# Gate loads four chunks sooner, and sparse work paced over the output phase's first chunks too

## The chip, the cores and the metric

The kernel runs on one core of one Trainium2 chip, as one launch. The metric is device microseconds of that launch. Three runs of the kernel before took 1379.41, 1379.86 and 1382.35 us; their median is 1379.86 us. All arithmetic is in float32 (matmuls on split float32r parts).

## The reference, cut to what matters

One encoder block: a mixer (gated convolution beside a recurrent scan), then a product-key expert layer, then a final normalization. The change lies wholly in the expert layer:

```python
def block(xb):                                  # 128 tokens at a time, 512 in all
    q = (xb @ w_q).reshape(p, PEER_HEADS, 2, PEER_DK_HALF)
    sc = jnp.einsum('phcd,hcnd->phcn', q, sub_keys)
    top_s, top_i = lax.top_k(sc, PEER_TOPK)
    ...
    g = jax.nn.softmax(best_s, axis=-1)
    u_sel = expert_u[idx]
    act = jax.nn.gelu(jnp.einsum('phkd,pd->phk', u_sel, xb), approximate=False)
    coef = (g * act.astype(jnp.float32)).astype(xb.dtype)
    return jnp.einsum('phk,phkd->pd', coef, expert_v[idx])
```

There are 16384 experts, and each token selects 128 of them (8 heads, 16 each). `expert_u` and `expert_v` have 16384 rows of 1024 numbers, 64 MB each.

## The kernel before

**Two ways to the experts.** The last 320 of the 512 tokens are done densely: every expert's activation is computed by matmul, in chunks of 128 experts. `u` chunk c gives `act` for those 320 tokens (24 matmuls of 320 columns, three per 128 rows of the model dimension since both sides are split into a high and a low part). `v` chunk n multiplies the coefficients of its 128 experts, 384 tokens wide, with 128 rows of `expert_v` (18 matmuls of 512 columns: three token blocks, two halves of the output, three split products) and accumulates over all 128 chunks in PSUM. The first 128 tokens (and, for the `u` side, 64 more) are done sparsely: for each of 128 selections a gather on GpSimd's queue (`gath`, L804-L807) fetches one expert row per token, 512 KB in all, into a ring of row buffers, and VectorE makes of it a dot product (`dots`, L828, on the `u` side) or a weighted sum (`sums`, L844, on the `v` side). One such instruction with its gather is a sparse step here. The ring has 5 buffers, and two more from some point in the output phase (`row_tile`, L795-L799), so gathers run four to six rows ahead of the step that uses them.

**Gates.** The softmax weights of the dense tokens are scattered beforehand into per-tile DRAM arrays `Gd[1..3]`, and `v` chunks read them back, 16 chunks at a time: three loads of 1 MB each, in pieces of 1 KB, one per token tile t (`load_g16`, L922-L937). The chunks 0 to 15 use a buffer `gt`. The chunks 16 to 31 use the memory of `h2`, the split normalized activations that the `u` chunks read; it is free once the last `u` chunk has been multiplied. The later groups of 16 alternate between the two.

**The order of the work.** The kernel writes the order out by hand, job by job. A list `jobs` holds `u` chunks 0 to 123, then `v0, u124, v1, u125, v2, u126, v3, u127, v4, v5, ...` (L852-L856). What follows `u123` is called the output phase here; its loop is L1104-L1131. At job k it asks for the weight chunk of job k+5 (`w_load`, 512 KB on SyncE's queue, the tile `wraw`, four buffers), splits the chunk of k+3 into its high part on ScalarE (`w_high`, the tile `whi`, L75) and of k+2 into its low part on VectorE (`w_low`, the tile `wlo`, L80); in a `v` job it then calls `v_gates(n + 5)` for the gates, on even n `v_act` and `v_gated` (L962, the coefficients `cf` of the next chunk pair, their high part `ch` on ScalarE), on odd n `v_rest` (the low part `cl` on VectorE, L980), issues the 18 matmuls, and last some sparse steps. The queue of SyncE is worked off in order, as are ScalarE and VectorE. Every weight load waits for the buffer's last reader, the `w_low` four jobs before it.

**When the gates are asked for.** `v_gates(n)` starts, for tile t, the load of the group that begins at chunk m = n + 4 - t while n < 16, and m = n + 13 - 3t after that (L951). For the group that begins at 16 this is at n = 13, 14 and 15, so in the jobs of the chunks 8, 9 and 10.

**How many sparse steps.** After `v` chunk n, steps are taken until their number reaches `share` (L1128). With 207 steps still to do at the loop's start (`steps`), NE = 128, VE = 1, QV = 3 and RB = 32 it is

share = min(max(n + 1 - 3, 0) / 124, 1) x (207 + 0.31 x 96) - 0.31 x max(n - 31, 0),

so none in the first three chunks, then a constant number per chunk, and 0.31 fewer per chunk from chunk 32 on, where spilled activations are loaded back too.

Of the kernel before, what the change touches and what calls it, by code (L numbers as in the profile page):

```python
# [21 lines left out]
NE = 128  # L22
# [12 lines left out]
def block_kernel(ctx, tc, xT, small, w_ada1, w_ada, b_ada, w_in, w_r, w_i, w_out, w_q, keys, uT, u, v, final_g, out):  # L35
# [825 lines left out]
    def w_load(k):  # L861
        if k < len(jobs):
            kind, i = jobs[k]
            if 5 <= k < FN:
                raw = wring.tile([128, KB, 128], FR, name=("wlo", "whi")[k % 2], bufs=WB).bitcast(F32)
                nc.sync.dma_start(raw, uT[i])
                wraw[k] = raw
                return
            wraw[k] = load_w(uT[i] if kind == "u" else
                             v[vorder[i] * 128:(vorder[i] + 1) * 128, :].rearrange("p (k e) -> p k e", k=KB))  # L870

    def w_high(k):
        if FN <= k < len(jobs):
            whi[k] = high(wraw[k])

    def w_low(k):
        if FN <= k < len(jobs):
            wlo[k] = low(wraw.pop(k), whi[k])
# [14 lines left out]
    def u_evict():  # L893
        if unread:
            c, ps = unread.pop()
            if c % 2 == 0:
                act[c // 2] = ring.tile([128, 2, NU], F32, name="act", bufs=RB // 2)
            nc.scalar.activation(act[c // 2][:, c % 2], ps, AF.Gelu)  # L898

    def u_chunk(k, pool):  # L900
        c = jobs[k][1]
        if c:
            ps = pool.tile([128, NU], F32, name="ps_act", bufs=2)
            if k < FN:
                raw = wraw.pop(k)
                for j in range(KB):
                    nc.tensor.matmul(ps, raw[:, j, :], h2f[j // 2][:, j % 2], start=j == 0, stop=j == KB - 1)
            else:
                mm3(ps, whi.pop(k), wlo.pop(k), hd, ld, range(KB), True, True)
            u_evict()  # L910
            unread.append((c, ps))
        q = c // 2 - RB // 2 + 2
        if c % 2 == 0 and 0 <= q < v0 // 2:
            spill(q)
        pe[0] += FPE if c and k < FN else 3530
        dve[0] += 0 if c and k < FN - 2 else 1140
        ac[0] += 450 if c and k < FN - 3 else 1400
# [4 lines left out]
    def load_g16(m, t):  # L922
        if m not in g16:
            if m % 32:
                big = g16[16] if m > 16 else persist.tile([128, 32, 16, 16], F32, name="h2")[:, 0:NG]
            else:
                big = gt8.rearrange("p s g i t -> p (s g i t)").rearrange("p (g i t) -> p g i t", i=16, t=16)
            g16[m] = big
            for k in range(0, 16, 2):
                gbuf[m + k] = big[:, :, k:k + 2, :]  # L930
        for k in range(0, 16, 8):
            cc = vorder[m + k]
            if k == 0 and vorder[m + 8] == cc + 8:
                nc.sync.dma_start(g16[m][:, 8 * t - 8:8 * t], Gd[t][:, :, cc:cc + 16, :].rearrange("g j i t -> j g i t"))
                return
            nc.sync.dma_start(g16[m][:, 8 * t - 8:8 * t, k:k + 8],
                              Gd[t][:, :, cc:cc + 8, :].rearrange("g j i t -> j g i t"))  # L937

    def v_gates(n):
        if n >= NE or n in gdone:  # L940
            return
        gdone.add(n)
        cc = vorder[n]
        if n < 16 and n % 8 == 0:
            gt = gt8[:, n // 8]
            for t in (2, 3, 1):
                nc.sync.dma_start(gt[:, 8 * t - 8:8 * t], Gd[t][:, :, cc:cc + 8, :].rearrange("g j i t -> j g i t"))
            for k in range(0, 8, 2):
                gbuf[n + k] = gt[:, :, k:k + 2, :]
        for t in range(1, NT):  # L950
            m = n + (4 - t if n < 16 else 13 - 3 * t)  # L951
            if m >= 16 and m % 16 == 0 and m < NE:
                load_g16(m, t)

    def v_act(q):
        if q < NE // 2:
            c = vorder[2 * q] // 2
            if act[c] is None:
                act[c] = ring.tile([128, 2, NU], F32, name="act", bufs=RB // 2)
                nc.sync.dma_start(act[c].rearrange("p c t -> p (c t)"), Ad[c])  # L960

    def v_gated(q):  # L962
        if q < NE // 2:
            cf = vp.tile([128, 2, ND], F32, name="cf", bufs=1)
            g = gbuf.pop(2 * q)
            nb = XB // 16
            nc.scalar.activation(cf[:, :, 0:XB].rearrange("p c (g t) -> p c g t", t=16),
                                 g[:, 0:nb].rearrange("p g c t -> p c g t"), AF.Copy)
            nc.vector.tensor_mul(cf[:, :, XB:].rearrange("p c (g t) -> p c g t", t=16),  # L969
                                 act.pop(vorder[2 * q] // 2).rearrange("p c (g t) -> p c g t", t=16),  # L970
                                 g[:, nb:].rearrange("p g c t -> p c g t"))
            ch = vp.tile([128, 2, ND], FR, name="ch", bufs=2)
            nc.scalar.activation(ch, cf, AF.Copy)  # L973
            coef[q] = (cf, ch)

    def v_rest(q):
        if q < NE // 2:
            cf, ch = coef[q]
            cl = vp.tile([128, 2, ND], FR, name="cl", bufs=2)
            nc.vector.tensor_sub(cl, cf, ch.bitcast(F32))  # L980
            coef[q] = (ch, cl)
# [36 lines left out]
    for k in range(CE):  # L1018
# [13 lines left out]
        while dve[0] < RHO * pe[0] or k == KD:  # L1032
# [7 lines left out]
            n = next(gens[g], 0)  # L1040
# [20 lines left out]
        m = k - CE + XE  # L1061
        if 0 <= m < XE:
            for n in [0] if m < 2 else range(5) if m == XE - 1 else [8]:
                v_gates(n)
# [17 lines left out]
    def v_chunk(n, b):  # L1082
        hi, lo, ch, cl = vsp[n]
        bs = slice(b * 128, (b + 1) * 128)
        for st, mv, first, last in ((ch, hi, n == 0, False), (ch, lo, False, False), (cl, hi, False, n == NE - 1)):
            for e in range(2):
                nc.tensor.matmul(accs[b][e], st[:, bs], mv[:, e * 512:(e + 1) * 512], start=first, stop=last)  # L1087
# [15 lines left out]
    steps, done = len(usteps) - len(bdone) + 128, 0  # L1103
    for k in range(CE, len(jobs)):  # L1104
        w_load(k + 5)
        w_high(k + 3)
        w_low(k + 2)
        kind, n = jobs[k]
        if kind == "u":
            u_chunk(k, psP)  # L1110
        else:
            q, e = divmod(n, 2)
            v_gates(n + 5)
            if e == 0:
                v_act(q + 4)
                v_gated(q + 1)
            else:
                v_rest(q + 1)
            vsp[n] = [w.pop(k).rearrange("p k e -> p (k e)") for w in (whi, wlo)] + [c[:, e] for c in coef[q]]
            if n < NE - VT:  # L1120
                for b in range(3):
                    v_chunk(n, b)
                del vsp[n]
            u_evict()
            pe[0] += 4090
            dve[0] += 2005
        if kind == "v":
            share = min(max(n + 1 - QV, 0) / (NE - VE - QV), 1) * (steps + 0.31 * (NE - RB)) - 0.31 * max(n + 1 - RB, 0)  # L1128
            while done < share and next(sparse, None):
                done += 1  # L1130
    fin = vp.tile([128, 2, 3, D], F32, name="gt", bufs=1)  # L1131
# [50 lines left out]
VE = 1  # L1182
# [5 lines left out]
CE = 124  # L1188
GB_E = 5
DR = 1.1  # L1190
QU = 6
QV = 3
RB = 32
ZL = 1
XE = 5
# [52 lines left out]
```

## Time and profile before

| | us |
|---|---|
| median of three runs | 1379.86 |
| the profiled execution | 1382.99 |
| its span, first to last instruction | 1381.1 |
| TensorE busy | 1325.2 (96%) |
| VectorE busy | 1222.7 (89%) |
| ScalarE busy | 700.7 (51%) |
| GpSimd busy | 528.9 (38%) |
| HBM read and written | 393.54 MB and 45.09 MB, 318 GB/s over the span |
| first matmul of `v` chunk 0 | 808.75 |

The profile is one execution. "Idle before" is time in which an engine did nothing ahead of an instruction, and the name behind the arrow is what that instruction waited for last. Matmuls are pipelined, each recorded longer than the distance to the next, so TensorE's loss is read from the distances and not from its busy share. "DMA share" is the busy time of packets over 16 DMA engines; it goes a little over 1 where packets overlap. q0 is the queue of GpSimd's gathers, q1 that of SyncE's loads and stores. In this profile and in what follows, `h` is the tile name under which the memory of `h2` appears.

### The profile page before, as it was taken

How to read it: one execution, taken by the hardware profiler on the slowest of the kernel's cores; microseconds unless marked ns; L12 is line 12 of the kernel's file. 1: busy time of each engine (PE TensorE's matmuls, PEld its weight loads, DVE VectorE, ACT ScalarE, POOL GpSimd, SP SyncE). 2: the span in 40 equal slices, each digit the busy share in tenths (PEclk: the TensorE clock that was granted, in tenths of full speed). 3: DMA queues.
4: the chain of work that ended last, by engine and by line, in shares of the span. 5: the costliest groups of instructions: out<-in, count | busy, mean ns of one | idle time of the engine just before them, and what ended most of it. 6: DMA issues, size and time to landing. Idle time of an engine off the chain costs nothing.

```text
span 1381.1 us, 21224 instructions
## 1 busy us (share of the span) xinstructions
PE 1325.2 (96%) x7483; PEld 1126.6 (82%) x7483; DVE 1222.7 (89%) x2302; ACT 700.7 (51%) x1199; POOL 528.9 (38%) x334
## 2 busy tenths in 40 slices
PE   5999999999999999999999999899999999999995
PEld 2666787777989999999999998787878887787884
DVE  6887766989999999999998649799999989898998
ACT  4666635424686887788644343333343434343442
POOL 0000000000242543435423406577656667576760
PEclk9999999999999999999999999999999999999998
DMA  9776332250699999999999988999999999999994
GB/s 352 253 265 217 126 93 99 69 184 31 215 317 347 343 412 331 363 334 407 417 397 336 406 260 283 407 393 416 413 414 412 415 413 414 411 415 412 409 377 164
DMA packets 146926, 440.03 MB, mean 319 GB/s; under 512 B 14722, under 2 KB 42370, under 8 KB 144772
## 3 DMA queue, kind: packets, MB, share of 16 engines
q1 hardware_dynamic: 99812, 267.75, 52.1%
q0 software_dynamic: 46720, 169.89, 31.4%
q8 instruction: 58, 0.95, 0.3%
q10 hardware_dynamic: 288, 1.05, 0.2%
q14 instruction: 48, 0.39, 0.1%
HBM read 393.54 MB, written 45.09 MB: 318 GB/s over the span
## 4 chain that ended last, share of the span: by engine, by line
DVE 32%; PE 21%; issue 21%; DMA 18%; ACT 4%; POOL 2%; DVEq 0%; SPq 0%; POOLq 0%; ACTq 0%
DMA wraw<-in_v_dram 14%; DVE wlo L80 7%; DVE scr L828 6%; PE ps_z L89 5%; PE ps_z L90 5%; PE ps_z L91 5%; DVE ys L844 3%; DMA wraw<-in_uT_dram 2%; DVE oh L667 2%; POOL rows L807 2%; DVE cf L969 2%; DVE cl L980 2%; ACT whi L75 1%; ACT igh L683 1%; PE ps_row L135 1%
## 5 line engine op out<-in xcount | busy, mean ns | idle before, releaser
L75 ACT ACTIVATE whi<-wraw 128x1024 fp32r<-128x1024 f32 x281 | 297.1, 1057 | 357.7 <-DMA wraw<-in_v_dram 192.8
L80 DVE TENSOR_TENSOR wlo<-wraw,whi 128x1024 fp32r<-128x1024 f32 x281 | 342.9, 1220 | 84.3 <-ACT whi L75 83.3
L89 PE MATMUL ps_act<-h,whi 128*128 128x320 f32 x928 | 293.8, 317 | 5.6 <-ACT act L898 5.6
L91 PE MATMUL ps_act<-h,wlo 128*128 128x320 f32 x928 | 288.1, 310 | 0.8 <-DVE wlo L80 0.8
L90 PE MATMUL ps_act<-h,whi 128*128 128x320 f32 x928 | 288.0, 310 | 0.0
L807 POOL DMA_INDIRECT rows<-in_u_dram,idx_s x128 | 192.5, 1504 | 213.6 <-DVE scr L828 183.4
L807 POOL DMA_INDIRECT rows<-in_v_dram,idx_s x128 | 225.5, 1762 | 107.4 <-DVE ys L844 82.5
L1087 PE MATMUL acc<-whi,ch 128*128 128x512 f32 x750 | 233.0, 392 | 7.6 <-ACT ch L973 7.1
L1087 PE MATMUL acc<-whi,cl 128*128 128x512 f32 x750 | 233.4, 392 | 5.7 <-DVE cl L980 5.6
L1087 PE MATMUL acc<-wlo,ch 128*128 128x512 f32 x750 | 231.9, 390 | 0.0
L807 POOL DMA_INDIRECT rows<-in_u_dram,idx_b x64 | 105.7, 1651 | 235.0 <-DVE scr L828 112.2
L89 PEld LDWEIGHTS ps_act<-h,whi 128*128 128x128 f32 x928 | 175.6, 189 | 7.8 <-ACT act L898 6.6
L91 PEld LDWEIGHTS ps_act<-h,wlo 128*128 128x128 f32 x928 | 175.4, 189 | 1.0 <-DVE wlo L80 1.0
L90 PEld LDWEIGHTS ps_act<-h,whi 128*128 128x128 f32 x928 | 175.6, 189 | 0.2
L1087 PEld LDWEIGHTS acc<-whi,ch 128*128 128x128 f32 x750 | 140.8, 189 | 39.0 <-ACT ch L973 9.4
L1087 PEld LDWEIGHTS acc<-whi,cl 128*128 128x128 f32 x750 | 140.3, 188 | 39.5 <-DVE cl L980 10.8
L1087 PEld LDWEIGHTS acc<-wlo,ch 128*128 128x128 f32 x750 | 141.4, 189 | 29.7
L844 DVE SCALAR_TENSOR_TENSOR ys<-rows,acts,ys 128x1024 f32<-128x1024 f32 x127 | 162.7, 1281 | 1.7
L828 DVE SCALAR_TENSOR_TENSOR scr<-rows,h2n 128x1024 f16<-128x1024 f32 x128 | 156.2, 1221 | 1.7 <-DMA rows<-in_u_dram,idx_s 0.2
L898 ACT ACTIVATE act<-ps_act 128x320 f32<-128x320 f32 x127 | 54.9, 432 | 139.5 <-PE ps_act L91 101.6
L683 ACT ACTIVATE igh<-oh,gl 128x128 f16<-128x128 f16 x320 | 99.7, 432 | 20.7 <-DVE oh L667 20.5
L433 POOL DMA_DIRECT2D x1d<-xn x8 | 4.5, 569 | 258.5 <-ACT xn L432 258.5
(284 smaller groups left out, 1837.2 us busy)
## 6 DMA issues: line engine op xcount, KB each, us to landing
wraw<-in_v_dram SPq DMA_DIRECT2D x128, 512.0 KB
wraw<-in_uT_dram SPq DMA_DIRECT2D x121, 512.0 KB
Gd<-stg SPq DMA_DIRECT2D x46, 512.0 KB
wada<-in_w_ada_dram SPq DMA_DIRECT2D x16, 1024.0 KB
Ad<-act SPq DMA_DIRECT2D x48, 320.0 KB
act<-Ad SPq DMA_DIRECT2D x48, 320.0 KB
h<-Gd SPq DMA_DIRECT2D x12, 1024.0 KB
wraw<-in_w_in_dram SPq DMA_DIRECT2D x20, 512.0 KB
```

The source lines that it names most:

```text
L75: nc.scalar.activation(hi, raw, AF.Copy)
L80: nc.vector.tensor_sub(lo, raw, hi.bitcast(F32))
L89: nc.tensor.matmul(ps, hi[:, k, :], xh(k), start=first and k == ks[0], stop=False)
L90: nc.tensor.matmul(ps, hi[:, k, :], xl(k), start=False, stop=False)
L91: nc.tensor.matmul(ps, lo[:, k, :], xh(k), start=False, stop=last and k == ks[-1])
L667: nc.vector.tensor_tensor(flat.rearrange("p (q n b) -> p q n b", q=8, b=2), io2[:, None, :, :].to_broadcast(shp), sij[:, a0].rearrange("p ...
L683: nc.scalar.activation(ig[:, 1, k // 2, :, k % 2], of[:, k // 2, 0, :, k % 2], AF.Copy, scale=gl[:, t0 + k:t0 + k + 1])
L807: nc.gpsimd.indirect_dma_start(out=r[:, :], out_offset=None, in_=table, in_offset=bass.IndirectOffsetOnAxis(ap=idxs[:, k:k + 1], axis=0))
L828: nc.vector.scalar_tensor_tensor(scr, rows.pop(n), 1.0, hn, op0=OP.mult, op1=OP.mult, accum_out=dst[:, k:k + 1])
L844: nc.vector.scalar_tensor_tensor(ys, rows.pop(k), acts[:, k:k + 1], ys, op0=OP.mult, op1=OP.add)
L898: nc.scalar.activation(act[c // 2][:, c % 2], ps, AF.Gelu)
L1087: nc.tensor.matmul(accs[b][e], st[:, bs], mv[:, e * 512:(e + 1) * 512], start=first, stop=last)
```

## The change

The gates for chunks 16 to 31, which go into the memory of `h2`, are asked for at n = 9, 10 and 11, so in the jobs of the chunks 4, 5 and 6. The group's later successors are asked for where they were. The sparse share begins with chunk 0; while a `u` chunk still stands between two `v` chunks (the first NE - CE = 4), each chunk counts as 1.86, and the whole counts 127 + 0.86 x 4 = 130.44.

```diff
         for t in range(1, NT):
-            m = n + (4 - t if n < 16 else 13 - 3 * t)
+            m = n + (8 - t if n < 16 else 13 - 3 * t)
             if m >= 16 and m % 16 == 0 and m < NE:
                 load_g16(m, t)
...
         if kind == "v":
-            share = min(max(n + 1 - QV, 0) / (NE - VE - QV), 1) * (steps + 0.31 * (NE - RB)) - 0.31 * max(n + 1 - RB, 0)
+            paced = n + 1 + UV * min(n + 1, NE - CE)
+            share = min(paced / (NE - VE + UV * (NE - CE)), 1) * (steps + 0.31 * (NE - RB)) - 0.31 * max(n + 1 - RB, 0)
             while done < share and next(sparse, None):
                 done += 1
...
-QV = 3
+UV = 0.86
```

The order of TensorE's instructions does not change. On SyncE, at the start of the output phase, the queue before reads (`wraw` are weight chunks, `h` the memory of `h2`, `Gd` the gates in DRAM, `gt` the other gate buffer):

```order
L70 DMA wraw<-in_uT_dram 128x1024
L70 DMA wraw<-in_v_dram 128x1024 x10
L934 DMA h_9519<-Gd_2592 128x8x256
L70 DMA wraw<-in_v_dram 128x1024
L934 DMA h_9519<-Gd_2593 128x8x256
L70 DMA wraw<-in_v_dram 128x1024
L934 DMA h_9519<-Gd_2594 128x8x256
L70 DMA wraw<-in_v_dram 128x1024 x7
L934 DMA gt<-Gd_2592 128x8x256
```

After the change the same stretch, from the same last `u` load to the same `gt` load, reads:

```order
L70 DMA wraw<-in_uT_dram 128x1024
L70 DMA wraw<-in_v_dram 128x1024 x6
L934 DMA h_9424<-Gd_2592 128x8x256
L70 DMA wraw<-in_v_dram 128x1024
L934 DMA h_9424<-Gd_2593 128x8x256
L70 DMA wraw<-in_v_dram 128x1024
L934 DMA h_9424<-Gd_2594 128x8x256
L70 DMA wraw<-in_v_dram 128x1024 x11
L934 DMA gt<-Gd_2592 128x8x256
```

The three loads of gates have moved ahead of four weight loads; six weight chunks (v4 to v9) stand ahead of the first of them now, and v10 and v11 between them. The loads behind keep their order.

On VectorE, from the coefficients of the second pair of chunks (`cf` of the jobs of v0) on, before:

```order
L969 TENSOR_TENSOR cf<-act,gt 128x2x320
L80 TENSOR_TENSOR wlo<-wraw,whi 128x1024 x2
L980 TENSOR_TENSOR cl<-cf,ch 128x768
L80 TENSOR_TENSOR wlo<-wraw,whi 128x1024 x2
L969 TENSOR_TENSOR cf<-act,gt 128x2x320
L80 TENSOR_TENSOR wlo<-wraw,whi 128x1024 x2
L980 TENSOR_TENSOR cl<-cf,ch 128x768
L828 SCALAR_TENSOR_TENSOR scr,acts<-rows,h2n 128x1024 x2
L80 TENSOR_TENSOR wlo<-wraw,whi 128x1024 x2
```

And after:

```order
L969 TENSOR_TENSOR cf<-act,gt 128x2x320
L828 SCALAR_TENSOR_TENSOR scr,acts<-rows,h2n 128x1024 x4
L80 TENSOR_TENSOR wlo<-wraw,whi 128x1024 x2
L980 TENSOR_TENSOR cl<-cf,ch 128x768
L828 SCALAR_TENSOR_TENSOR scr,acts<-rows,h2n 128x1024 x3
L80 TENSOR_TENSOR wlo<-wraw,whi 128x1024 x2
L969 TENSOR_TENSOR cf<-act,gt 128x2x320
L828 SCALAR_TENSOR_TENSOR scr,acts<-rows,h2n 128x1024 x4
L80 TENSOR_TENSOR wlo<-wraw,whi 128x1024 x2
L980 TENSOR_TENSOR cl<-cf,ch 128x768
L828 SCALAR_TENSOR_TENSOR scr,acts<-rows,h2n 128x1024 x3
L80 TENSOR_TENSOR wlo<-wraw,whi 128x1024 x2
```

Fourteen dot products stand behind the first four `v` chunks where two stood; each takes a gather with it, as a row buffer comes free. The steps that follow come correspondingly thinner: the total is the same.

## The prediction

> **What bounds the kernel now.** Only the output phase, from 808.75 us on, is touched. I read first the table of stretches, because the change moves work between them. Its columns are length, busy time and instructions of TensorE, its weight loads, VectorE, ScalarE and GpSimd, then granted clock, DMA share and GB/s.
>
> ```profile
> 810.00:835.00 25.00, 25.00 (x137) 22.47 (x136) 13.22 (x14) 10.48 (x14) 1.80 (x1) 1.00 0.60 203
> 835.00:860.00 25.00, 25.00 (x121) 21.28 (x120) 22.70 (x32) 9.88 (x14) 16.73 (x11) 1.00 0.88 307
> 860.00:885.00 25.00, 20.60 (x91) 16.79 (x90) 17.82 (x26) 6.42 (x9) 14.77 (x10) 0.97 1.04 411
> 885.00:900.00 15.00, 15.00 (x55) 12.06 (x55) 13.81 (x21) 6.24 (x9) 7.80 (x5) 0.82 0.97 366
> 900.00:963.00 63.00, 61.89 (x269) 49.85 (x268) 60.85 (x85) 22.77 (x29) 47.16 (x28) 1.00 1.03 412
> 963.00:1300.00 337.00, 329.74 (x1441) 269.12 (x1440) 313.75 (x317) 126.42 (x161) 224.56 (x130) 1.00 1.03 413
> 1300.00:1381.00 81.00, 66.27 (x292) 54.22 (x290) 76.93 (x106) 28.53 (x48) 32.44 (x19) 0.94 0.75 292
> ```
>
> The reader sees a DMA system that is full (1.03, 412 to 413 GB/s) from about 855 us to 1300 us, and that stood at 203 GB/s from 810 to 835. Next, the pace that TensorE could keep, from its timeline in `v4`, where nothing is late, with the end of `u127` ahead of it:
>
> ```profile
> 839.17 0.31 PE L91 MATMUL ps_act<-h,wlo 128*128 128x320 f32 x1
> 839.32 0.63 PE L1087 MATMUL acc<-whi,ch 128*128 128x512 f32 x2
> 839.79 0.62 PE L1087 MATMUL acc<-wlo,ch 128*128 128x512 f32 x2
> ...
> 842.97 0.61 PE L1087 MATMUL acc<-whi,cl 128*128 128x512 f32 x2
> ```
>
> Between the last two rows lie 14 matmuls: 3.18 / 14 = 0.227 us each, 4.09 us for a chunk of 18. From 963 to 1300, 1441 / 18 = 80 chunks took 337 us, or 4.21 each: 80 x 4.09 = 327, so 10 us are lost there. From 900 to 963, 269 / 18 = 14.9 chunks should take 61.1: 1.9 us lost. The groups of 963 to 1300 tell on what:
>
> ```profile
> L807 POOL DMA_INDIRECT rows<-in_v_dram,idx_s x110 | 193.4, 1758 | 95.8 <-DVE ys L844 75.2 <-issue 12.5 <-DVE scr L828 7.9
> L1087 PE MATMUL acc<-whi,cl 128*128 128x512 f32 x480 | 148.9, 391 | 5.2 <-DVE cl L980 5.1
> ...
> L75 ACT ACTIVATE whi<-wraw 128x1024 fp32r<-128x1024 f32 x80 | 84.9, 1061 | 180.6 <-DMA wraw<-in_v_dram 156.1 <-PE acc L1087 22.1 <-issue 2.3
> ```
>
> ScalarE waits for weight chunks (156.1 us), not for TensorE (22.1): the loads come late, and TensorE loses a little behind them through `cl`. The stretch is set by bandwidth, with TensorE 3% below it.
>
> The one large stall stands in the timelines of ScalarE and TensorE:
>
> ```profile
> 870.81 1.06 ACT L75 ACTIVATE whi<-wraw 128x1024 fp32r<-128x1024 f32 x1 [4.40 <-DMA wraw<-in_v_dram]
> 871.78 0.23 ACT L816 ACTIVATE acts<-acts 128x64 f32<-128x64 f32 x1
> 882.52 1.06 ACT L75 ACTIVATE whi<-wraw 128x1024 fp32r<-128x1024 f32 x1 [10.51 <-DMA wraw<-in_v_dram]
> 883.49 0.29 ACT L967 ACTIVATE cf<-gt 128x128 f32<-128x128 f32 x1
> 883.81 0.84 ACT L973 ACTIVATE ch<-cf 128x768 fp32r<-128x768 f32 x1
> ```
>
> ```profile
> 884.71 1.22 PE L1087 MATMUL acc<-whi,ch 128*128 128x512 f32 x2 [4.40 <-ACT ch L973]
> ```
>
> Chunk 14 does not lack its own weights; `ch` is queued on ScalarE behind the split of chunk 15, whose load landed at 882.5. What was in the way shows in SyncE's queue and in the DMA queues from 867.5 to 877.5:
>
> ```profile
> 851.72 1.64 SPq L934 DMA_DIRECT2D h<-Gd  x1
> 855.91 0.33 SPq L70 DMA_DIRECT2D wraw<-in_v_dram  x1
> 856.29 0.43 SPq L934 DMA_DIRECT2D h<-Gd  x1
> 860.26 6.83 SPq L70 DMA_DIRECT2D wraw<-in_v_dram  x1
> 867.14 1.58 SPq L934 DMA_DIRECT2D h<-Gd  x1
> ```
>
> ```profile
> q0 software_dynamic: 863, 3.15, 76.9%
> q1 hardware_dynamic: 879, 0.98, 27.1%
> ```
>
> v14 (855.91) and v15 (860.26) each stand behind a gate load. The queues alternate one packet for one (863 to 879): gathers come in 4 KB packets, gates in 1 KB, so the gathers took 3.15 MB and the gates' queue 0.98. The stall cost 4.40 us idle, and at a clock of 0.82 for 15 us another 0.18 x 15 = 2.7: 7.1 us together.
>
> **The Trainium skill on this.** "DMA: Bandwidth & Descriptors", section on queues, rings and completion order, says that an engine drains a whole packet of some 9 to 17 descriptors before it turns to the other queue. By that the gates would not pay four times over; the counts of 863 to 879 do not bear it out for these transfers, if its packets are the profile's. An estimate by that rule: no stall would follow the gates, and the sum would be that of the first rival below, 17 us. "TensorE: Matmul & The Clock Gate", Part 1, says that an idle window of about 3.4 us halves the clock; the 0.82 behind 4.40 us agrees, and by it a stall of 2 or 3 us would mostly be spared the 2.7; as an estimate by that page, the gain on the stall would be some 2 us more than I take.
>
> **The change part by part.** First the *sparse pace*. Left to do in the phase are
>
> ```profile
> L844 DVE SCALAR_TENSOR_TENSOR ys<-rows,acts,ys 128x1024 f32<-128x1024 f32 x127 | 162.7, 1281 | 1.7
> ...
> L828 DVE SCALAR_TENSOR_TENSOR scr<-rows,h2n 128x1024 f16<-128x1024 f32 x79 | 96.5, 1221 | 1.4 <-DMA rows<-in_u_dram,idx_s 0.2
> ```
>
> 79 dots and 128 sums (the first sum is another operation), 207 steps. With 0.31 x 96 = 29.8 the share counts 236.8. Before: 236.8 / 124 = 1.91 per chunk, and 1.60 from chunk 32 (the trace has 130 gathers for 80 chunks). After: 236.8 / 130.44 = 1.815 and 1.505, and 1.86 x 1.815 = 3.38 in each of the first four. So each chunk from the fifth on carries 0.094 gathers less, and the first four carry them all. A gather moves as much as a weight chunk:
>
> ```profile
> wraw<-in_v_dram SPq DMA_DIRECT2D x128, 512.0 KB
> ...
> h<-Gd SPq DMA_DIRECT2D x12, 1024.0 KB
> ```
>
> 512 KB at 413 GB/s is 1.27 us of all DMA; 0.094 x 1.27 = 0.12 us per chunk. From 963 to 1300: 80 x 0.12 = 9.5 of the 10 us lost. 4.21 - 0.12 = 4.09 is just TensorE's pace, so neither has slack and unevenness stays: I take 7, bounds 2 and 10. From 900 to 963, 15 x 0.12 = 1.8 of 1.9 lost; VectorE is at 60.85 of 63 there and sheds 0.094 x 1.22 = 0.11 us a chunk too: I take 1, bounds 0 and 2.
>
> Where does the moved work go? Into this hole in GpSimd's timeline:
>
> ```profile
> 786.31 0.94 POOL L807 DMA_INDIRECT rows<-in_u_dram,idx_s  x1 [0.31 <-issue]
> 832.99 1.80 POOL L807 DMA_INDIRECT rows<-in_u_dram,idx_s  x1 [45.74 <-DVE scr L828]
> ```
>
> VectorE's room there:
>
> ```profile
> 808.00:837.00 29.00, 28.47 (x155) 25.36 (x154) 13.52 (x15) 11.92 (x16) 2.73 (x2) 1.00 0.62 204
> ...
> 852.00:884.00 32.00, 28.31 (x125) 23.10 (x124) 24.60 (x36) 8.77 (x13) 21.16 (x15) 0.99 1.03 402
> ```
>
> 15.5 us free besides two dots, against 14 dots of 1.22 = 17.1 with those two (2.4) counted in: 17.9 available. It just fits, and weights run a chunk or two ahead there, so I put it at nothing; if it spills over it costs up to 2 us. A pair of chunk and `u` chunk holds 3.38 dots on the mean; the `x4` ones push the next `wlo` late, the `x3` ones give it back.
>
> Then the *gates*. SyncE reaches the first after v9, about 835, and must wait for `u127`'s last matmul, 839.3 by the row above; v10 queues behind that wait for a microsecond or so, on a buffer lead of many. Then two 1 MB loads stand ahead of v11. For chunk 10 to start on time (839.3 + 6 x 4.09 = 863.9), v11 must land 2.2 us earlier (882.52 to 884.71 above), so within 22.3 us. Queue q1's own work to there: per engine 64 packets a gate load; q1's 27.1% of 10 us over 879 / 16 packets is 0.049 us each, so 3.1 us a load: 2 x 3.1 + 2 x 1.27 = 8.7. That leaves 13.6 us, 10.7 gathers. The steps ask for 1.815 x 22.3 / 4.09 = 9.9, plus what is left over from before 839: of 29 us since 810, q1 needs 203 x 25 / 413 = 12.3 and one more load, 13.6; 15.4 remain for 12 of the 14 gathers and the two with which the row ring grows. Some 3 remain, so v11 is late by (9.9 + 3 - 10.7) x 1.27 = 2.8 us. The same reckoning of the old stall (26.4 us from 851.7, three weights and two gates 10.0, so 12.9 gathers, against the 15 of 852 to 884 above) gives 2.7 where 4.4 was measured; scaled so, 4.5. The stall moves to chunk 10 to 12 and shrinks from 7.1 to about 4 us: I take a gain of 3, bounds -4 and +7.
>
> Behind the phase, 1300 on, nothing changes: both paces reach the same total at chunk 126.
>
> **Sum**: 3 + 1 + 7 = 11 us. It cannot exceed the DMA time left idle that it fills, 25 x (413 - 203) / 413 + 25 x (413 - 307) / 413 = 19. The profiled execution took 1382.99 us (1381.1 span and 1.9 around it), 3.1 above the median of 1379.86; the loss it shows may be a little above the median run's. 1382.99 - 11 = 1372.0; on the median, 1369.
>
> **The rivals.** What a measurement can tell from no change here is about 0.2%, 2.8 us.
>
> *Both losses go.* If gathers are not backed up at 839, or gates are served by more than a packet a turn, the gates pass in 3.1 us each and no stall follows: 7 + 2 + 8 = 17, 1363. The first rule of the Trainium skill above ("DMA: Bandwidth & Descriptors") speaks for this one. For it: gathers never make VectorE wait now (0.2 us above). Against it: the one-for-one counts. Chance 0.12.
>
> *The stall only moves, and takes the gain along (slower).* If the gathers moved forward keep q0 backed up through all three gate loads, each takes 64 x (0.049 + 0.143) = 12.3 us (0.143: 76.9% of 10 us over 863 / 16). v11 would land at 839.3 + 2 x 12.3 + 2 x 2.5 = 869, 7 late, and v13 some 17 us after, 9 more than two chunks give: 16 idle with the clock's 2.7, against 7.1 before: +12, less 8 later, +4: 1384. It decides at some 24 gathers waiting in 40 us, where the pace supplies 18 and the leftover 3. Chance 0.08.
>
> *Bandwidth is not what the later stretch lacks (no change).* If the losses of 963 to 1300 come from bunching (a gate load, two act loads and gathers at once), 6% fewer gathers leave them, and the early stall is as long as before: gain 0 to 2.5, 1378. For it: the lost 10 us are few and scattered. Against it: 1.03 throughout, 156.1 us of waits on weights. Chance 0.12.
>
> **The numbers.** The forecast has 0.68, its own range 1364 to 1375. Faster by over 0.2%: 0.68 + 0.12 = 0.80; within: 0.12; slower: 0.08. The range goes from 1361, 2 us under the best rival for the uncertainty of a median, to the no-change case's 1378; it leaves out the slower one and edges.
>
> **What would show it.** Right: no whole idle of 4 us at chunk 14; 810 to 835 near 400 GB/s; a stall of 2 to 4 us at chunks 10 to 12; 80 chunks from chunk 32 on in about 330 us; whi's wait for weights well below 156. Wrong: a stall over 5 us behind the gates, TensorE waiting in the first four chunks, or an unchanged pace of 4.2 us a chunk with fewer gathers.

## The result, and the profile after

The changed kernel takes 1370.03 us (median of six runs, 1366.3 to 1371.44), the kernel before 1379.84 (six runs, 1379.4 to 1382.35). The ratio is 0.9915, with a 95% interval of 0.9901 to 0.9929. In a later session it was 0.9907 (0.9892 to 0.9921). The forecast was 1369. Of the kernels tried further below, three executions (2194.7, 3370.89 and 3371.16 us) ran in a much slower state and stand in none of the ratios.

The profiled execution took 1370.00 us against 1382.99. Of these 13.0 us, 2.0 lie ahead of the output phase (its first matmul stands at 806.73 instead of 808.75) and 1.1 behind the last matmul, where the program is the same; the output phase itself shrank from 558.0 to 548.2 us, by 9.8, which is also the difference of the medians. The table of stretches after:

```profile
810.00:835.00 25.00, 25.00 (x140) 22.65 (x139) 23.72 (x32) 10.06 (x13) 15.83 (x14) 1.00 1.00 381
835.00:860.00 25.00, 25.00 (x118) 21.09 (x117) 19.90 (x28) 6.86 (x11) 13.53 (x10) 1.00 1.04 410
860.00:885.00 25.00, 23.14 (x95) 18.49 (x94) 22.74 (x32) 10.53 (x14) 16.61 (x11) 0.93 1.00 384
885.00:900.00 15.00, 15.00 (x68) 12.44 (x67) 14.90 (x22) 6.22 (x8) 11.68 (x8) 1.00 0.98 358
900.00:963.00 63.00, 61.66 (x271) 50.41 (x270) 60.18 (x83) 22.79 (x29) 45.30 (x27) 1.00 1.03 415
963.00:1300.00 337.00, 332.60 (x1464) 274.09 (x1463) 309.07 (x303) 128.73 (x165) 213.69 (x124) 1.00 1.03 406
1300.00:1368.00 68.00, 54.90 (x243) 45.13 (x241) 64.13 (x94) 24.02 (x42) 22.03 (x13) 0.92 0.71 274
```

The hole is filled: 810 to 835 moves 381 GB/s instead of 203, with VectorE at 23.72 us of 25 instead of 13.22 and no loss on TensorE. From 963 to 1300, 1464 matmuls fit where 1441 did, and 124 gathers instead of 130. One sign that the prediction named did not come: it had ScalarE's wait for weight chunks in that stretch well below 156 us, and it is

```profile
ACT whi L75 <- DMA wraw<-in_v_dram: 143.4, 54, 9.0
```

The stall behind the gate loads is now at chunk 10, as ScalarE's and TensorE's timelines show:

```profile
855.12 1.06 ACT L75 ACTIVATE whi<-wraw 128x1024 fp32r<-128x1024 f32 x1 [7.30 <-DMA wraw<-in_v_dram]
861.64 1.06 ACT L75 ACTIVATE whi<-wraw 128x1024 fp32r<-128x1024 f32 x1 [5.45 <-DMA wraw<-in_v_dram]
862.60 0.29 ACT L967 ACTIVATE cf<-gt 128x128 f32<-128x128 f32 x1
862.93 0.84 ACT L973 ACTIVATE ch<-cf 128x768 fp32r<-128x768 f32 x1
```

```profile
861.35 0.61 PE L1087 MATMUL acc<-whi,cl 128*128 128x512 f32 x2
863.82 0.73 PE L1087 MATMUL acc<-whi,ch 128*128 128x512 f32 x2 [1.85 <-ACT ch L973]
864.39 0.62 PE L1087 MATMUL acc<-wlo,ch 128*128 128x512 f32 x2
864.88 0.73 PE L1087 MATMUL acc<-whi,cl 128*128 128x512 f32 x2
865.45 1.02 PE L1087 MATMUL acc<-whi,ch 128*128 128x512 f32 x2
```

v11's weights land at 861.6, and `ch` for chunk 10 waits behind them. TensorE idles about 2 us, and from 865.45 on two matmuls take 0.8 us instead of 0.45: the clock of 0.93 over 25 us is another 1.75 us. SyncE's queue shows the cause as forecast, two gate loads on either side of v10, and v11 behind both:

```profile
834.74 0.33 SPq L70 DMA_DIRECT2D wraw<-in_v_dram  x1
837.49 0.38 SPq L934 DMA_DIRECT2D h<-Gd  x1
837.96 0.54 SPq L70 DMA_DIRECT2D wraw<-in_v_dram  x1
838.55 1.06 SPq L934 DMA_DIRECT2D h<-Gd  x1
840.62 9.82 SPq L70 DMA_DIRECT2D wraw<-in_v_dram  x1
```

For all kernels below the loss is counted the same way: the time from the first matmul of one `v` chunk to that of another in TensorE's timeline, less 18 x 0.227 = 4.086 us per chunk (and 24 x 0.147 for a `u` chunk between). "Phase" is from the first matmul of v0 to the end of the last one. All in us, each from one profiled execution; the ratios are those of the timed runs to the kernel before in the same session, with their intervals.

| kernel | loss of chunks 4-16 | 16-32 | 32-112 | phase | GB/s, 810 to 835 | ratio |
|---|---|---|---|---|---|---|
| before | 7.4 | 2.3 | 10.3 | 558.0 | 203 | |
| changed | 3.9 | 1.9 | 5.2 | 548.2 | 381 | 0.9915 (0.9901 to 0.9929) |
| changed, again | 4.0 | 3.4 | 2.7 | 547.4 | 389 | 0.9907 (0.9892 to 0.9921) |
| gates sooner alone | 6.6 | 3.7 | 10.2 | 559.2 | 153 | 1.0009 (0.9997 to 1.0021) |
| new pace alone | 0.0 | 4.6 | 5.6 | 547.5 | 372 | 0.9908 (0.9895 to 0.9922) |
| half of each v row | 6.9 | 3.0 | 2.7 | 549.9 | 154 | 0.9946 (0.9928 to 0.9965) |
| gates on ScalarE's queue | 4.5 | 0.4 | 9.0 | 551.2 | 365 | 0.9973 (0.9959 to 0.9988) |
| ring grows late, old pace | 1.2 | 5.4 | 16.2 | 560.1 | 167 | 0.9998 (0.9989 to 1.0007) |
| UV = 0 | 5.4 | 2.0 | 7.6 | 552.2 | 306 | 0.9939 (0.9925 to 0.9952) |
| UV = 1.6 | 10.6 | -0.1 | 0.4 | 548.3 | 365 | 0.9919 (0.9903 to 0.9935) |
| gates spread, new pace | 0.6 | 1.7 | 3.9 | 543.6 | 361 | 0.9881 (0.9865 to 0.9897) |
| gates spread, old pace | 1.5 | 5.2 | 9.9 | 554.9 | 155 | 0.9966 (0.9952 to 0.9979) |
| gates spread, UV = 1.2 | 1.8 | 1.1 | 1.8 | 542.0 | 379 | 0.9863 (0.9844 to 0.9881) |

No kernel lost over 0.2 us in the chunks 0 to 4.

### The profile page after: what moved, and what is told of

The parts are those of the page before. It is cut to its first block, busy times and chain, and to the rows that moved or that the text cites. A ratio compares the mean times of both kernels' runs of the same rounds, so it can differ in the third digit from the quotient of the medians.

```text
span 1368.2 us, 21234 instructions
## 1 busy us (share of the span) xinstructions
PE 1319.1 (96%) x7483; PEld 1127.0 (82%) x7483; DVE 1222.0 (89%) x2302; ACT 700.3 (51%) x1199; POOL 525.4 (38%) x334
## 4 chain that ended last, share of the span: by engine, by line
PE 46%; DVE 25%; issue 14%; DMA 10%; POOL 3%; ACT 2%; DVEq 0%; SPq 0%; POOLq 0%; ACTq 0%
PE acc L1087 15%; DMA wraw<-in_v_dram 7%; PE ps_z L89 5%; PE ps_z L90 5%; PE ps_z L91 5%; DVE scr L828 4%; DVE wlo L80 4%; PE ps_act L89 4%; PE ps_act L91 4%; PE ps_act L90 4%; POOL rows L807 3%; DVE ys L844 2%; DVE oh L667 2%; DVE cl L980 2%; DVE cf L969 1%
## 5 line engine op out<-in xcount | busy, mean ns | idle before, releaser
L844 DVE SCALAR_TENSOR_TENSOR ys<-rows,acts,ys 128x1024 f32<-128x1024 f32 x127 | 162.8, 1282 | 1.5
```

The source lines that it names most:

```text
L844: nc.vector.scalar_tensor_tensor(ys, rows.pop(k), acts[:, k:k + 1], ys, op0=OP.mult, op1=OP.add)
```

## The experiments

**Each half of the change alone.** The theory was that two gains add: 3 us from the gates' place, 8 from the pace. The rivals were that the one or the other is the whole.

```diff
-            m = n + (4 - t if n < 16 else 13 - 3 * t)
+            m = n + (8 - t if n < 16 else 13 - 3 * t)
```

(gates sooner alone, on the kernel before.) 

> The kernel before with the gate loads at chunks 4 to 6 and the old sparse pace. Theory (two causes that add: the stall at chunk 14 comes from two gate loads ahead of a weight load while gathers compete, the later loss from bandwidth): with the old pace almost no gathers run before chunk 4, so none is left over at 839 us; v11 has 10.7 gathers' room and 10.4 are asked for, so no stall over 1 us at chunks 10 to 16, the clock stays at 1.0, and the stretch of chunks 32 to 112 still takes about 337 us: 5 to 7 us under the kernel before, 1373 to 1375. Rival (the gates' place in the queue is the whole of it): 1370 or less. Rival (the pace is the whole of it): 1379 to 1381.

```diff
-            m = n + (8 - t if n < 16 else 13 - 3 * t)
+            m = n + (4 - t if n < 16 else 13 - 3 * t)
```

(new pace alone, on the changed kernel.) 

> The changed kernel with the gate loads back at chunks 8 to 10. Theory of two causes: chunks 32 to 112 take 331 to 333 us as in the changed kernel (5 us less than before), and a stall of 2 to 6 us remains at chunks 12 to 14: 1372 to 1376. Rival (the gates' place is the whole of it): 1379 to 1381. Rival (the pace is the whole): 1370.

Gates sooner alone took 1382.24 us, a ratio of 1.0009 (0.9997 to 1.0021); the new pace alone 1367.9, 0.9908 (0.9895 to 0.9922), which is the changed kernel's 0.9915 within the intervals. As far as these intervals tell (about 2 us), the pace is the whole. Both expected times were missed. With the gates sooner alone the stall did not vanish, it moved from chunk 14 to chunk 12, and the clock stood at 0.86 from 860 to 885:

```profile
872.60 1.22 PE L1087 MATMUL acc<-whi,ch 128*128 128x512 f32 x2 [2.99 <-ACT ch L973]
```

With the new pace alone, put at 1372 to 1376, no stall came at the chunks 12 to 14 either. It came at chunk 16, with a loss of 3.9 us:

```profile
887.00 0.98 PE L1087 MATMUL acc<-whi,cl 128*128 128x512 f32 x2 [2.04 <-DVE cl L980]
```

GpSimd's gathers are one candidate for the reason. The rows are the six chunks that begin when the gate loads are asked for: before (chunks 8 to 14), gates sooner alone (4 to 10), changed (4 to 10) and new pace alone (8 to 14).

```profile
855.70:880.20 24.50, 18.22 (x13) 1.00 1.04 412
```

```profile
836.80:861.30 24.50, 18.51 (x13) 1.00 1.01 387
```

```profile
837.30:861.80 24.50, 13.21 (x9) 1.00 1.04 408
```

```profile
851.20:875.70 24.50, 15.11 (x10) 1.00 1.04 408
```

With the old pace 13 gathers are issued while the gate loads run, wherever these stand; with the new one it is 9 or 10. But the count of issues does not settle it, because gathers issued earlier are still on their way. What the gathers' queue moved in the same windows was 5.15 MB with gates sooner alone and 5.61 MB in the changed kernel:

```profile
q0 software_dynamic: 1418, 5.15, 51.5%
```

```profile
q0 software_dynamic: 1549, 5.61, 56.1%
```

The kernel with the longer stall moved less. So why the early move fails under the old pace is argued here and not shown. My reckoning for chunk 4 took the new pace's 9.9 and its leftover and compared it with the old place's 15; it never asked what the old pace does at the new place.

**Is it bandwidth later on?** Half the bytes of each `v` gather, at the same work on every engine:

```diff
-            nc.gpsimd.indirect_dma_start(out=r[:, :], out_offset=None, in_=table,
+            w, src = (D // 2, v.rearrange("e (h d) -> (e h) d", h=2)) if table is v else (D, table)
+            nc.gpsimd.indirect_dma_start(out=r[:, :w], out_offset=None, in_=src,
...
+            twice = rows.pop(k)[:, None, :D // 2].to_broadcast([128, 2, D // 2])
+            y2 = ys.rearrange("p (h d) -> p h d", h=2)
...
-                nc.vector.scalar_tensor_tensor(ys, rows.pop(k), acts[:, k:k + 1], ys, op0=OP.mult, op1=OP.add)
+                nc.vector.scalar_tensor_tensor(y2, twice, acts[:, k:k + 1], y2, op0=OP.mult, op1=OP.add)
```

> The kernel before, but each of the 128 gathers on the v side fetches half a row (512 numbers, of a wrong place), and VectorE reads this half twice, so its work is as long as before; the sums are those of other numbers. Theory (bandwidth sets the later stretch): 256 KB less for 1.6 gathers a chunk is 1 us of DMA per chunk, so once the sums have begun (chunk 44) every chunk takes 4.09 to 4.10 us, GB/s falls under 340, and some 7 to 8 us are saved: 1371 to 1373. Rival (bunching of a gate load, activation loads and gathers, whatever their sum): stalls with each group of gates remain, 1376 to 1379. Rival (VectorE sets it): no change, 1379 to 1381.

It took 1373.45 us, 0.9946 (0.9928 to 0.9965). Its stretches, while dots are still made and after the sums have begun, and what ScalarE and GpSimd wait for in the latter:

```profile
963.00:1030.00 67.00, 65.17 (x283) 52.41 (x282) 61.76 (x84) 24.75 (x32) 43.08 (x27) 1.00 1.02 401
1030.00:1300.00 270.00, 270.00 (x1193) 223.58 (x1192) 263.45 (x244) 104.80 (x133) 184.72 (x108) 1.00 0.92 323
```

```profile
ACT whi L75 <- PE acc L1090: 157.4, 65, 3.0
POOL rows L808 <- DVE ys L847: 72.8, 66, 2.8
```

From 1030 on TensorE loses nothing, and the waits for weights, 156.1 us before over the whole of 963 to 1300, have turned into waits for TensorE. The bytes were the cause; with the same gate loads and activation loads, and a weighted sum as long as before (1282 ns against 1281), there is no bunching left to see. The bandwidth theory holds, and the rivals fall.

**The gates out of the weights' queue.**

```diff
-                nc.sync.dma_start(g16[m][:, 8 * t - 8:8 * t], Gd[t][:, :, cc:cc + 16, :].rearrange("g j i t -> j g i t"))
+                nc.scalar.dma_start(g16[m][:, 8 * t - 8:8 * t], Gd[t][:, :, cc:cc + 16, :].rearrange("g j i t -> j g i t"))
...
-                nc.sync.dma_start(g16[m][:, 8 * t - 8:8 * t, k:k + 8],
+                nc.scalar.dma_start(g16[m][:, 8 * t - 8:8 * t, k:k + 8],
```

> The changed kernel with the gate loads from chunk 16 on issued on ScalarE's DMA queue, so that no weight load stands behind one; same bytes, same times of asking. Theory (the stall that is left, 3.9 us at chunk 10, is the weight load's place behind two gate loads, and the four late stalls of 1 to 2 us, 16 chunks apart, are the same): early stall under 1 us, no late stall over 0.7 us, 4 to 8 us under the changed kernel: 1362 to 1366. Rival (total bandwidth is what is short, whoever waits): within 2 us of the changed kernel, 1368 to 1372. Rival (a gate load waiting on ScalarE for h2's last reader holds up the splits queued behind it): slower than the changed kernel by 1 to 3 us, with ScalarE late at chunk 4.

1377.19 us, 0.9973 (0.9959 to 0.9988): slower than the changed kernel by some 8 us, where the third answer allowed 1 to 3. ScalarE's timeline shows a hold that none of the answers named:

```profile
848.33 1.06 ACT L75 ACTIVATE whi<-wraw 128x1024 fp32r<-128x1024 f32 x1 [2.88 <-PE acc L1087]
848.33 9.92 ACTq L934 DMA_DIRECT2D h<-Gd  x1
858.30 0.31 ACT L967 ACTIVATE cf<-gt 128x128 f32<-128x128 f32 x1 [8.91 <-issue]
```

The third gate load is being issued for 9.92 us, and ScalarE does nothing meanwhile. On SyncE the same thing (9.82 us in the rows of the changed kernel) holds up loads only. The hold does not explain the 8 us, though: the chunks 4 to 16 lose 4.5 us, and 3.9 in the changed kernel. The larger loss is late, 9.0 us in the chunks 32 to 112. Of these 5.4 fall on chunk 80, and there ScalarE waits for a weight chunk as in the other kernels:

```profile
1147.35 1.06 ACT L75 ACTIVATE whi<-wraw 128x1024 fp32r<-128x1024 f32 x1 [7.24 <-DMA wraw<-in_v_dram]
```

So the run does not decide what the queue's order costs, and the cause of its time stays open.

**What makes the stall.** A new theory: the row ring grows by two buffers at its 128th gather, and the gathers that fill it fall on the gate loads. In GpSimd's queue before, eight gathers are issued from 853.60 to 864.71, where VectorE's pace asks for some five. In the old pace the growth was moved later, and nothing else:

```diff
-            late[:] = [gp, taken[0] + 10]
+            late[:] = [gp, taken[0] + 45]
```

> The kernel before, with the two extra row buffers taken into use 35 gathers later (about chunk 27 in place of chunk 9); pace and gate loads as before. New theory: the early stall is as long as the number of gathers that compete with the gate loads, and in the kernel before the ring's growth (8 gathers in 11 us, some 3 more than VectorE's pace asks for) falls right on them; the new pace moves the growth ahead of the gates, their place in the queue does nothing. Then the loss of the chunks 4 to 16 falls from 7.3 to 2 to 4 us here and the whole by 3 to 5 us against the kernel before, if the growth does no harm at chunk 27. Rival (the rate of 1.91 against 1.815 gathers a chunk makes the difference, not the growth): loss of 6 to 8 us at chunks 4 to 16, and no change of the whole. Rival (a ring of five is too short while the gates pass): longer stall, slower than the kernel before.

The time did not change: 0.9998 (0.9989 to 1.0007). One more execution gave the profile that the table shows.

> A second look, for a profile, at the kernel before with the ring's growth 35 gathers later, which took as long as the kernel before. If the growth had nothing to do with the early stall: the chunks 4 to 16 lose 6 to 8 us, as before. If the gain was given back: they lose 2 to 4 us, and the chunks 24 to 48, where the ring grows now, 3 to 5 us more than the 3 to 4 of before.

That execution took 1382.23 us. Six chunks from 853.7 on carry 11 gathers instead of 13, and the chunks 4 to 16 lose 1.2 us instead of 7.4. So in this execution the stall of the kernel before went when the growth went. But the 6 us come back in the chunks 16 to 112, which lose 21.6 instead of 12.6:

```profile
963.00:1300.00 337.00, 328.04 (x1418) 268.53 (x1417) 310.89 (x313) 125.27 (x159) 217.15 (x129) 0.98 1.03 412
```

The DMA system is as full as before, 1418 matmuls stand where 1441 did, and stalls there have cost some clock as well (0.98). As a theory of the time, the growth falls: here a stall of 7 us was not 7 us to be had. Why is not fully told apart: the chunks 24 to 48, among which the ring grows now, lose 8.6 us instead of 5.7, so a part of what came back may be harm that the growth does at its new place.

**How much early work.** UV was set to 0 and to 1.6.

```diff
-UV = 0.86
+UV = 0.0
```

> The changed kernel with UV = 0: steps begin with chunk 0, but the chunks with a u chunk between count as one; 1.86 a chunk, 1.55 from chunk 32, about 7 steps instead of 14 behind the first four chunks. Bandwidth theory: about half of the later gain, so the chunks 32 to 112 lose 7 to 8 us (10.3 before, 5.2 changed); the growth of the ring comes at chunks 5 to 7, on the gate loads, so the chunks 4 to 32 lose 7 to 9 us as in the kernel before: 3 to 5 us under the kernel before. Rival (only the earlier start matters, not how much of it): 8 to 11 us under the kernel before.

```diff
-UV = 0.86
+UV = 1.6
```

> The changed kernel with UV = 1.6: 4 to 5 steps behind each of the first four chunks, 1.775 a chunk after them and 1.465 from chunk 32. VectorE then needs 2.44 for two wlo, 0.89 for cf or cl and 4.6 x 1.22 = 5.6 for the steps, 8.9 us, where a pair lasts 7.62. Theory (VectorE's room there just covered 14 steps): TensorE loses 2 to 4 us in chunks 0 to 8, the chunks 32 to 112 lose 3 to 4 us instead of 5.2, and the whole is within 2 us of the changed kernel, 1368 to 1373. Rival (weights run far enough ahead to cover it, DMA has room): 2 to 4 us under the changed kernel.

With UV = 0 the chunks 32 to 112 lose 7.6 us, between the two kernels as expected; the whole came out at 1374.51 us, 0.9939 (0.9925 to 0.9952), 7 us under the kernel before where 3 to 5 were expected. With UV = 1.6 it is 1369.95, 0.9919 (0.9903 to 0.9935), no different from the changed kernel, but for two effects that cancel. Late, it loses 0.4 us in 80 chunks:

```profile
963.00:1300.00 337.00, 336.66 (x1484) 278.13 (x1484) 311.97 (x301) 131.31 (x168) 202.87 (x123) 1.00 1.03 412
```

Early, it has a stall of the kind that the rival with the chance of 0.08 describes; that gathers backed up behind the gate loads make it is not shown:

```profile
862.11 0.61 PE L1087 MATMUL acc<-whi,cl 128*128 128x512 f32 x2
868.95 1.22 PE L1087 MATMUL acc<-whi,ch 128*128 128x512 f32 x2 [6.22 <-ACT ch L973]
```

The expected loss on VectorE, 2 to 4 us in the chunks 0 to 8, came too, but behind the first four. The chunks 0 to 4 lose 0.1 us, and 5 and 6 lose 2.4: VectorE works there without a gap, and TensorE waits for `cl` behind the steps.

```profile
847.01 0.73 PE L1087 MATMUL acc<-whi,cl 128*128 128x512 f32 x2 [1.44 <-DVE cl L980]
```

**The gate loads apart from each other**, at chunks 4, 7 and 10, under the new pace, under the old one, and with UV = 1.2:

```diff
-            m = n + (8 - t if n < 16 else 13 - 3 * t)
+            m = n + (10 - 3 * t if n < 16 else 13 - 3 * t)
```

> The changed kernel with the three gate loads at chunks 4, 7 and 10 in place of 4, 5 and 6. Theory (a weight load that lands late stands behind two gate loads): only one stands ahead of any weight load for three chunks, so the chunks 4 to 16 lose under 1.5 us in place of 3.9, with no half clock behind it: 2 to 4 us under the changed kernel, 1366 to 1368. Rival (it is the sum of all bytes until chunk 16): loss of 3 to 5 us somewhere in the chunks 4 to 20, as in the changed kernel.

> The kernel before with the three gate loads at chunks 4, 7 and 10, old pace. Theory (the early stall needs two gate loads ahead of one weight load): the chunks 4 to 16 lose under 2 us in place of 7.3 without any change of pace, the chunks 32 to 112 lose about 10 as before: 3 to 6 us under the kernel before. Rival (without the pace the gathers crowd in from chunk 4 on, 14 of them until chunk 10 where the new pace has 9, and one gate load ahead is enough): loss of 4 to 7 us at chunks 4 to 32, at most 3 us under the kernel before.

> New pace with UV = 1.2 and the gate loads at chunks 4, 7 and 10: 16 steps behind the first four chunks, 1.795 a chunk after them and 1.485 from chunk 32. Theory (bandwidth later, VectorE and gate loads early): the chunks 32 to 112 lose under 2 us, the chunks 0 to 16 lose 1 to 4 us more than with 0.86 and gates spread, so within 2 us of that kernel: 1365 to 1368. Rival (early room is left): 1362 to 1364.

> The changed kernel itself beside the spread gates of this call, on the same chip. If the gain of the spread gates is real: 2 to 5 us above the kernel with UV = 1.2 and spread gates; a loss of 3 to 5 us at chunks 4 to 16 again, and 3 to 7 us at chunks 32 to 112, which tells how much of that stretch differs from one execution to the next.

Under the new pace it took 1366.52 us, 0.9881 (0.9865 to 0.9897), and 0.6 us are lost in the chunks 4 to 16: at this pace one gate load ahead of a weight load did next to no harm, and two did. Under the old pace, 1377.35, 0.9966 (0.9952 to 0.9979): the stall goes there too (1.5), as the theory has it, but the chunks 16 to 32 lose 5.2 instead of 2.3, and only about 3 us of the phase come out of it. With 6.7 us in the chunks 4 to 32 the rival's loss came as well. With UV = 1.2, 1363.75, 0.9863 (0.9844 to 0.9881), against 1369.3 for the changed kernel in the same session. Of the expectations, 1365 to 1368 was too slow and 1362 to 1364 held. This is the fastest kernel tried by its median. It is clear of the changed kernel; against spread gates with UV = 0.86 the intervals overlap, so that the extra early work gains anything is not shown. Its later stretch has next to no loss:

```profile
963.00:1300.00 337.00, 336.22 (x1481) 277.38 (x1480) 312.50 (x303) 130.59 (x166) 210.18 (x124) 1.00 1.03 411
```

Why a stall that goes can pay a little all the same may lie in what it does to the DMA system: it holds VectorE, VectorE frees no row buffers, and the gathers stop. Behind its stall, the kernel with gates sooner alone shows

```profile
860.00:885.00 25.00, 21.19 (x83) 16.58 (x82) 17.03 (x23) 8.12 (x11) 13.10 (x9) 0.86 0.91 342
```

and the one with spread gates and the old pace

```profile
860.00:885.00 25.00, 25.00 (x112) 20.71 (x111) 19.71 (x30) 6.48 (x9) 15.68 (x11) 1.00 1.03 416
```

25 x (416 - 342) / 413 = 4.5 us of DMA time were left idle by the bunched stall. That is the order of the 4.3 us between the two phases (559.2 and 554.9); that it is the whole reason was not tried.

The second profile of the changed kernel repeats the early loss (4.0) and shows a loss of 2.7 us in the chunks 32 to 112 where the first had 5.2; the kernel's median lies 5.6 us above that with UV = 1.2, where 2 to 5 were expected. A difference of 2 or 3 us there, from one profile each, is not to be read.

## Why the prediction was right, point by point

- **What bounds the phase.** Right: bandwidth from chunk 32 on was shown by taking bytes away.
- **The sparse pace, later stretch.** 7 us forecast (2 to 10); 5.1 and 7.6 in the two profiles (10.3 before, 5.2 and 2.7 after). Right in kind, and in size as far as two profiles can tell that differ by 2.5 us. With fewer gathers still (UV = 1.6) the loss goes to nothing, as the sum of bytes per chunk says.
- **900 to 963.** 1 us forecast; the matmuls went from 269 to 271, two of 0.227 us. Nothing to speak of.
- **VectorE's cover in the first four chunks.** Put at nothing, and it was: 23.72 us of 25, no loss on TensorE. With four to five steps a chunk (UV = 1.6) it no longer holds: 2.4 us are lost just behind.
- **The gates.** Place and size of the new stall were right: chunk 10, 2 us idle and 1.75 of clock, where about 4 in all was forecast. The working behind it came close as well: v11's split began 24.3 us after chunk 4 did (861.64 against 837.30), and 22.3 + 2.8 = 25.1 was forecast. The step that failed is the one that gave a gain of 3 to the gates' move. That move alone is worth nothing (1.0009), and the pace alone gives all of it (0.9908). I had worked out the old stall at the old place and the new one at the new place, and never the old pace at the new place. That fewer gathers are issued beside the gate loads, 9 or 10 instead of 13, goes with the pace and not with the place; whether this is what shortens the stall stays open. The terms came out as 3.5, 0.4 and 5.1 in the first profile, with 0.8 more around the last chunks, 9.8 in all, and as 3.4, -1.1 and 7.6 in the second. So it is partly luck that the sum of 11 stands near the measured 9.8: one term had the wrong owner, and the pace's own part in the early stall was missing.
- **The bound on the whole.** The prediction's bound of 19 us counts the DMA time left idle from 810 to 860. Of it 25 x (381 - 203) / 413 = 10.8 and 25 x (410 - 307) / 413 = 6.2 were filled, 17.0 together. Later less was moved than before: by 1.6 from 860 to 885, 0.3 to 900 and 5.7 from 963 to 1300, with 0.5 more from 900 to 963. That leaves 9.9 for the gain. Since both kernels move the same bytes, this account has to close whatever the cause is, and it proves none. The first 25 us alone come near the gain too (10.8; 10.2 for the pace alone, with 10.5 in its phase; 6.2 for UV = 0, with 5.8). But with the gates on ScalarE's queue the same count gives 9.8 for a phase shorter by 6.8, and with the gates spread 9.6 for 14.4. It is no rule.
- **The rivals.** "Bandwidth is not what the later stretch lacks" fell. "The stall only moves, and takes the gain along" is real, but shows with UV = 1.6, where it pays for itself, and in the gates' move alone. "Both losses go" was put at 1363. The early loss goes with the gates spread (0.6 us are left), which the rival did not name; that kernel's 0.9881 is 1363.4 us on the scale of the first session. Of the rival's own conditions, more than a packet a turn is not borne out by the counts that follow.

On the alternation of the queues, from 845 to 860 in the changed kernel:

```profile
q0 software_dynamic: 923, 3.32, 54.2%
q1 hardware_dynamic: 2066, 2.78, 49.8%
```

Here the gates' queue got two packets for each of the gathers'. Two shorter windows show how, 842 to 844 and 854 to 856:

```profile
q0 software_dynamic: 172, 0.61, 74.2%
q1 hardware_dynamic: 202, 0.21, 29.0%
```

```profile
q1 hardware_dynamic: 580, 0.60, 84.4%
q0 software_dynamic: 56, 0.20, 25.0%
```

While gathers are under way it stays near one for one, 172 to 202; when their queue runs empty in between, the gates' queue gets nearly all, 580 to 56. That this is why the stall is shorter now is likely but was not tested. "DMA: Bandwidth & Descriptors" of the Trainium skill (queues, rings and completion order) speaks of 9 to 17 descriptors a turn; these counts cannot tell that apart from one a turn, since equal numbers from both queues come out one for one either way. For the same reason the prediction's estimate by that page does not follow: with equal numbers of rows a turn, rows of 1 KB still lose four for one to rows of 4 KB.

"TensorE: Matmul & The Clock Gate", Part 1, of the Trainium skill wants an idle window of about 3.4 us before the clock is halved. By it I would have spared a 2 us stall the cost. The measurement decides otherwise: the clock fell behind 1.85 us of idle (the row of 863.82 above, 0.93 over 25 us), and stayed at 1.00 behind 2.90 us in the kernel with spread gates, whose rows are

```profile
1004.32 0.73 PE L1087 MATMUL acc<-whi,ch 128*128 128x512 f32 x2 [2.90 <-ACT ch L973]
```

```profile
1001.00:1008.00 7.00, 4.11 (x17) 2.85 (x16) 4.75 (x5) 3.30 (x5) 1.22 (x1) 1.00 1.03 420
```

The page also says that the window runs free of the program. That could let one gap pass and catch another, but a whole window of 3.4 us does not fit into a gap of 1.85; so the page does not account for the first row, and no run here shows what does.

## What to carry to other kernels

Where a shared resource is full behind a stall, the length of the stall is not what its removal pays. With the bytes unchanged, shortening a 7 us stall of TensorE gained nothing in one kernel (the ring grown late) and about 3 us of the phase in another (the gates spread, old pace). Early work moved into a hole of the DMA system, on the other hand, lowered the load on everything behind it. Follow the idle time of the resource over the whole stretch, because a single window can agree by chance. When two edits come together, work out each alone at the other's old setting before giving it a share; a right sum can hide a wrong owner. Large loads that share an in-order queue with a stream of small deadlines are best put a few deadlines apart: at the changed kernel's pace, two in a row went with a loss of 4 us in the chunks 4 to 16, and one at a time with 0.6.

## What the runs showed of the hardware that was not expected

- A DMA issued from ScalarE held ScalarE for 9.92 us, with 8.91 us of idle ahead of its next instruction, where two earlier gate loads were still under way (of their 2 MB their queue had moved 0.24 MB when it began and 0.86 MB when it ended). On SyncE an issue took as long (9.82 us).
- The clock fell to half behind 1.85 us of idle TensorE in the changed kernel (0.50 from 865.50 to 868.90) and behind 2.04 us with the new pace alone (0.50 from 887.30 to 890.70), and not at all behind 2.90 us with spread gates.
- With rows of 1 KB on one queue and of 4 KB on the other, the packets went near one for one as long as both had some (525 to 524 from 870 to 876 in the kernel before).
